# One norm recorded ahead of attention, the last pairs' products in another order, and new planned costs for narrow matmuls, merges and norm sums

## The chip, the cores and the metric

The kernel runs on one core of a Trainium2 chip. The metric is the device time of one execution, in microseconds. The engines named here are TensorE (PE in the profile, its weight loads PEld), VectorE (DVE), ScalarE (ACT), GpSimd (POOL) and SyncE (SP), which issues the DMAs.

## The reference

A network of two layers on 1024 tokens with 1024 features, all in f32. Layer 0 mixes by attention over a sliding window of 128 tokens with a sink per head (16 query heads and 4 key heads of 64), layer 1 by an HGRN2 recurrence in chunks of 64 tokens (8 heads of 128). Each layer ends with an MLP of 4096 hidden features with a squared ReLU, and each part starts with an RMS norm.

```python
def rmsnorm(x, gain):
    xf = x.astype(jnp.float32)
    y = xf * lax.rsqrt(jnp.mean(jnp.square(xf), axis=-1, keepdims=True) + NORM_EPS)
    return (y * gain.astype(jnp.float32)).astype(x.dtype)

def sqrelu_mlp(h, w_up, w_down):
    return jnp.square(jax.nn.relu(h @ w_up)) @ w_down

    scores = jnp.where(mask[None, :, None, None], scores, NEG_INF)
    m = jnp.maximum(jnp.max(scores, axis=-1, keepdims=True), sink)
    e = jnp.exp(scores - m)
    probs = e / (jnp.sum(e, axis=-1, keepdims=True) + jnp.exp(sink - m))
    ...
        scores = jnp.einsum('bhtd,bhtsd,bhsd->bhts', qc, decay, kc)
        o_intra = jnp.einsum('bhts,bhse->bhte', scores, vc)
        new_state = jnp.exp(b_last)[..., None] * state + jnp.einsum(
            'bhsd,bhse->bhde', kc * jnp.exp(b_last[:, :, None, :] - b), vc)
        return new_state, o_inter + o_intra
    ...
    for layer in range(DEPTH):
        j = layer // N_MIXERS
        h = rmsnorm(x, mix_norm[layer])
        if layer % N_MIXERS == 0:
            y = sliding_window_attention(h, positions, attn_w_qkv[j], attn_b_qkv[j],
                                         attn_sinks[j], attn_w_o[j])
        else:
            y = hgrn2_recurrence(h, lbs[layer], hgrn_w_in[j], hgrn_g_norm[j], hgrn_w_o[j])
        x = x + y.astype(x.dtype)
        h = rmsnorm(x, mlp_norm[layer])
        x = x + sqrelu_mlp(h, mlp_w_up[layer], mlp_w_down[layer]).astype(x.dtype)
    return rmsnorm(x, final_norm)
```

## The kernel before, in words

**Work.** The tokens are held as two halves of 512, the features as 8 tiles of 128. A matmul of f32 data is three passes (`mm3`): each operand is split into a high part and a rest (tiles `wh` and `wl` of a weight, pairs of `a` of an activation), and high x high, high x rest and rest x high are summed in one PSUM bank. A split is a cast (on ScalarE or VectorE) and a subtraction (VectorE). PSUM has eight banks in two pools of four, `p` and `q`. Raw weights arrive in tiles `wr`, their sums stand in `m`, activations in `a` and `t`, small columns in `sm`.

**Order.** Every operation is first recorded in `Schedule` by `add` and only then issued. `due` (line 187) walks backward from the end and gives each operation a rank by its due time; `order` (line 205) then runs a list schedule: each engine, when free by the planned clock, takes the ready operation of the lowest rank. The planned clock is made of the cost that each operation is recorded with (`mm`, line 426, plans n * rate / 2.4 + 3 ns), a table of latencies between engines, and 120 ns where TensorE changes from whole matmuls to column matmuls. `lead` lets what is recorded under it rank earlier by 120 ns for each unit; `LEAD` is 100, so 12 us. A buffer of a pool is given to the next tile in recorded order when it is free by the plan. What results is one program per engine, which that engine works through in order. All operations are issued by one helper, so every line of the profile is L372, and tiles tell them apart.

**The MLP.** `pair` (line 643) takes two of the 16 steps of the upper product at a time, by seven products instead of eight (the rows and columns are combined first, in the way of Strassen). Each `product` is 12 matmuls of 128x512 for the half pair's tile. Products 1, 6, 7 and 4 add up in the bank main, 5 and 3 in the bank side (both of pool `q`), 2 alone in own (pool `p`). Between 1, 6, 7 and 4 the bank main is read (`read`, a copy into a `t` tile): u1, u2, u3; p5 is read from side. The hidden tiles that result are stored in DRAM. `down` (line 731) then loads them again (`t<-d`), splits them and multiplies them by the lower weights, three matmuls to a bank, eight banks in turn. Its first matmuls are free to go ahead of the last pair's last product.

**Attention.** `attention` (line 1059) scales and splits the first half, records its keys, values and queries (`qkv`), then the second half's scaling, and then `attend(0)` interleaved with `qkv(1)`. `scaled` returns the split tiles and a function that, when called, records the norm: eight squares (ScalarE), their sum (VectorE), and `token_rstd` (line 492): matmuls of the sum by a column of 1/1024, one for each block of 128 tokens (128x1 in the trace), the root on ScalarE, and some small VectorE operations. `qkv(1)` calls it at its first step.

**HGRN.** `recurrence` (line 1245) works on pairs of tokens' blocks inside a chunk, by levels: `products` (line 1269) issues narrow matmuls (32 or 64 columns wide) on halves of the array's columns, and `merge` (line 1278) puts their result into the scores by a predicated copy on VectorE.

Of the kernel before, what the change touches and what calls it, by code (L numbers as in the profile page):

```python
# [18 lines left out]
P = 128  # L19
# [6 lines left out]
MT = FF // P  # L26
# [9 lines left out]
BPH = NBLK // NH  # L36
# [6 lines left out]
CH = 64  # L43
# [93 lines left out]
LEAD = 100  # L137
# [181 lines left out]
class Net:  # L319
# [172 lines left out]
    def token_rstd(self, acc, inner=1.0, outer=1.0, n=TH, tag="q"):  # L492

        ps = self.psum(tag)
        nb = n // P
        for j in range(nb):
            self.mm(ps[:, j : j + 1], acc[:, j * P : j * P + P], self.mean, True, True, 64, 4)
        v, y, z = (self.t(F32, (P, BPH), "sm")[:, :nb] for _ in range(3))
        self.ts("DVE", v, ps[:, :nb], inner, EPS, ALU.mult, ALU.add, 4)
        self.act(y, v, AF.Sqrt, 4)  # L500
        self.op("DVE", self.nc.vector.reciprocal, [y], [y], 100, y, y)
        self.tt("DVE", z, y, y, ALU.mult, 4)
        self.tt("DVE", z, z, v, ALU.mult, 4)
        self.ts("DVE", z, z, -0.5 * outer, 1.5 * outer, ALU.mult, ALU.add, 4)
        self.tt("DVE", y, y, z, ALU.mult, 4)
        return y
# [136 lines left out]
    def pair(self, m, x):  # L643

        w = self.strassen_weights(*(self.io["up"][self.layer, i] for i in (m, m + MT // 2)))

        def read(ps):
            z = self.t()
            self.take(z, ps)
            return z  # L650

        main, side, own = self.psum("q"), self.psum("q"), self.psum()
        self.product(main, w[1], x[1], True)
        u1 = read(main)
        self.product(own, w[2], x[2], True)
        self.product(side, w[5], x[5], True)
        p5 = read(side)
        self.product(main, w[6], x[6], False)
        u2 = read(main)
        self.product(side, w[3], x[3], False)  # L660
        self.product(main, w[7], x[7], False)
        u3 = read(main)
        self.product(main, w[4], x[4], False)
        def kept(name, z):
            self.hid[name, m] = self.keep(z)

        self.add_bank(u1, own)
        h00 = self.square_relu(u1)
        kept(1, h00)
        self.add_bank(u2, side)  # L670
        h01, t5, t6, t4 = self.square_relu(u2), *(self.t() for _ in range(3))
        self.tt("any", t5, h01, h00, ALU.subtract)
        kept(5, t5)
        self.tt("any", p5, p5, u3, ALU.add)
        h11 = self.square_relu(p5)
        kept(3, h11)
        self.tt("any", t6, h11, t5, ALU.subtract)
        kept(6, t6)
        self.tt("any", h01, h11, h01, ALU.subtract)
        kept(7, h01)  # L680
        h10 = self.square_relu(main, True)
        kept(2, h10)
        self.tt("any", t4, h10, t6, ALU.subtract)
        kept(4, t4)
# [374 lines left out]
    def attention(self, layer):  # L1059
        self.v, self.dv, self.ks, self.kl = [], [], [None] * 3, [None] * 3  # L1060
        self.q = [[None] * 2 for _ in range(NBLK)]
        out = [{}, {}]
        self.load_x([0])
        h = [self.scaled(layer, 0)]
        self.attention_constants()
        run(self.qkv(0, *h[0]))
        self.load_x([1])
        h.append(self.scaled(layer, 1))
        interleave(self.attend(0, out[0]), self.qkv(1, *h[1]), 16, 24)
        interleave(self.attend(1, out[1]), self.o_proj(0, out[0]), 24, 8)  # L1070
        self.mlp_first(layer)
        run(self.o_proj(1, out[1]))
# [172 lines left out]
    def recurrence(self, e, ready, totals, out):  # L1245

        gates = ready.pop(e)
        NC = NH * BPH
        chunk = lambda z, j: z[:, j * CH : j * CH + CH]
# [4 lines left out]
        def parts(z, lg):  # L1254
            return z.rearrange("p (n a h) -> p n a h", a=2, h=1 << lg)

        def moved(lg):
            return [(k, [parts(chunk(q, j), lg)[:, :, 1] for j in range(2 * BPH)]) for q, f, k, g in gates]
# [10 lines left out]
        def products(part, operands, late, width=CH // 2):  # L1269
            part = part.rearrange("p (c t) -> p c t", c=NC)  # L1270
            for hf, (k, qs) in enumerate(operands):
                for c in range(BPH):
                    for b in range(2):
                        rows = slice(b * CH, b * CH + CH)
                        j = 2 * c + b
                        self.mm(part[rows, hf * BPH + c], chunk(k, j), qs[j], True, True, width, 2.06, "columns", late)

        def merge(part, lg):
            H = 1 << lg
            n = CH // (2 * H)  # L1280
            mask = parts(self.level_mask[lg], lg)[:, :, 1].unsqueeze(1).to_broadcast([P, NC, n, H])
            target = scores.rearrange("p c (n a h) -> p c n a h", a=2, h=H)[:, :, :, 1]
            part = part.rearrange("p (c n h) -> p c n h", c=NC, n=n)
            self.op("DVE", self.nc.vector.copy_predicated, [target], [mask, part], 70 + NC * CH // 2 * 1.04, target, mask, part)

        def views(operands):
            return [z for k, qs in operands for z in (k, *qs)]
# [8 lines left out]
        gates = decayed  # L1296
        late = views(plain) + views(moved(0))
        products(whole, plain, late, CH)
        products(half, moved(0), late)
        mask = self.diag.unsqueeze(1).to_broadcast([P, NC, CH])  # L1300
        self.tt("DVE", scores, whole.rearrange("p (c t) -> p c t", c=NC), mask, ALU.mult)
        merge(half, 0)
        yield
        for lg in range(1, LEVELS, 2):
# [5 lines left out]
            if lg < LEVELS - 1:  # L1310
                second = moved(lg + 1)
                late = views(first) + views(second)
                products(low, first, late)
                products(high, second, late)
                merge(low, lg)
                merge(high, lg + 1)
            else:
                late = views(first) + [z for q, f, k, g in gates for z in (q, k)]
                products(low, first, late)
                cross = self.psum("q")[:CH].rearrange("p (c t) -> p c t", c=NC)  # L1320
                for hf, (q, f, k, g) in enumerate(gates):
                    for c in range(BPH):
                        self.mm(cross[:, hf * BPH + c], chunk(k, 2 * c), chunk(q, 2 * c + 1), True, True, CH, 3.9, "columns", late)
                merge(low, lg)
                weights = []
                for hf in range(NH):
                    s, c = self.t(F32, (P, BPH, 2, CH)), slice(hf * BPH, hf * BPH + BPH)
                    self.memset(s[CH:, :, 0].only(0), 0.0, "Pool")
                    self.copy(s[:CH, :, 0].only(1), scores[:CH, c], 4 * CH)
                    self.copy(s[CH:, :, 1].only(2), scores[CH:, c], 4 * CH)  # L1330
                    self.copy(s[:CH, :, 1].only(3), cross[:, c], 4 * CH)
                    weights.append(s)
                at, tot = self.double(CH, gates, tot, tots, at)
# [149 lines left out]
def run(pieces):  # L1483
    for _ in pieces:
        pass


def interleave(main, other, n_main, n_other):
    done = 0
    for k, _ in enumerate(main):  # L1490
        while done * n_main < (k + 1) * n_other and next(other, run) is not run:
            done += 1
    run(other)
# [81 lines left out]
```

## Time and profile before

| | us |
|---|---|
| runs: 2004.93, 2006.69, 2010.59; median | 2006.69 |
| the profiled execution | 2007.87 |
| its span | 2005.5 |
| around the span | 2.37 |
| TensorE busy | 1979.5 |
| VectorE busy | 1699.2 |
| ScalarE busy | 1013.7 |
| mean granted clock of TensorE | 0.998 |

A row of the timeline gives start, length, engine, line, operation, the tile written, the tiles read, their shape, how many in a row, and in brackets the engine's idle time just ahead and who released it. Numbers behind tiles are left out there. A matmul's length in the trace is longer than the step from one to the next, since they overlap.

### The profile page before, as it was taken

The numbers are of one execution on the slowest core, as the hardware profiler recorded it, in microseconds if no ns is written. First come the engines' busy times: TensorE is split into PE (matmuls) and PEld (weight loads), VectorE is DVE, ScalarE is ACT, GpSimd is POOL, SyncE is SP. The second block draws the span as 40 slices with busy tenths as digits, with TensorE's granted clock in tenths as the row PEclk, the third lists the DMA queues.
The fourth block names the chain that finished last, engine by engine and source line by source line (L and its number), as shares of the span: only waits on it lengthen the run. The fifth ranks groups of instructions, "written<-read, shape, count | busy, mean of one in ns | idle before, by whom it ended". The sixth has DMA issues, their size and how long they took to land.

```text
span 2005.5 us, 32701 instructions
## 1 busy us (share of the span) xinstructions
PE 1979.5 (99%) x11404; PEld 1718.5 (86%) x11404; DVE 1699.2 (85%) x3360; ACT 1013.7 (51%) x2045; POOL 62.7 (3%) x124
## 2 busy tenths in 40 slices
PE   9999999999999999999999999999999999999998
PEld 8877788888888888888888888888888888888887
DVE  8999899777778878799898999989977777887787
ACT  6567796554454323255345555554654445323352
POOL 4030100000000000000000000000000000000001
PEclk9999999999999999999999999999999999999999
DMA  6212463544468967745422212667444446886752
GB/s 216 90 53 59 127 222 120 184 167 160 146 204 292 314 217 264 235 163 176 146 63 78 78 59 90 207 208 244 142 167 160 146 162 237 286 301 215 236 179 85
DMA packets 196677, 345.88 MB, mean 172 GB/s; under 512 B 21536, under 2 KB 31776, under 8 KB 196512
## 3 DMA queue, kind: packets, MB, share of 16 engines
q1 hardware_dynamic: 195936, 343.28, 52.0%
q8 instruction: 89, 1.46, 0.3%
q14 instruction: 76, 0.62, 0.1%
q10 hardware_dynamic: 576, 0.52, 0.1%
HBM read 250.39 MB, written 93.32 MB: 171 GB/s over the span
## 4 chain that ended last, share of the span: by engine, by line
PE 85%; DVE 7%; DMA 3%; issue 2%; ACT 2%; POOL 0%; SPq 0%; POOLq 0%; DVEq 0%; ACTq 0%
PE q L372 51%; PE p L372 34%; DVE t L372 3%; DVE a L372 2%; DVE wl L372 1%; ACT t L372 1%; ACT a L372 1%; DMA wr<-in_down 1%; DVE m L372 0%; DMA a<-in_x 0%; ACT wh L372 0%; ACT m L372 0%; DMA t<-d 0%; DMA wr<-in_wqkv 0%; DMA wr<-in_wv 0%
## 5 line engine op out<-in xcount | busy, mean ns | idle before, releaser
L372 PE MATMUL q<-a,wh 128*128 128x512 f32 x2560 | 761.8, 379 | 3.5 <-ACT t L372 3.5
L372 PE MATMUL p<-a,wh 128*128 128x512 f32 x2112 | 644.6, 383 | 0.1
L372 PEld LDWEIGHTS q<-a,wh 128*128 128x128 f32 x2560 | 482.3, 189 | 74.1 <-ACT t L372 5.0
L372 PE MATMUL q<-a,wl 128*128 128x512 f32 x1280 | 484.9, 379 | 0.0
L372 PEld LDWEIGHTS p<-a,wh 128*128 128x128 f32 x2112 | 394.2, 189 | 54.6 <-issue 1.2
L372 PE MATMUL p<-a,wl 128*128 128x512 f32 x1056 | 401.6, 381 | 0.0
L372 ACT CAST a<-t 128x512 fp32r<-128x512 f32 x283 | 172.0, 619 | 286.0 <-PE q L372 142.8
L372 PEld LDWEIGHTS q<-a,wl 128*128 128x128 f32 x1280 | 241.9, 189 | 34.3
L372 ACT ACTIVATE t<-t 128x512 f32<-128x512 f32 x272 | 171.1, 631 | 189.8 <-DVE t L372 182.2
L372 DVE TENSOR_TENSOR wl<-wr,wh 128x512 fp32r<-128x512 f32 x352 | 240.6, 686 | 11.7 <-ACT wh L372 3.9
L372 DVE TENSOR_TENSOR t<-t,t 128x512 f32<-128x512 f32 (+3 forms) x364 | 224.9, 638 | 26.8 <-ACT t L372 23.1
L372 PEld LDWEIGHTS p<-a,wl 128*128 128x128 f32 x1056 | 199.7, 189 | 26.8 <-issue 0.4
L372 DVE TENSOR_TENSOR a<-t,a 128x512 fp32r<-128x512 f32 (+1 forms) x326 | 217.2, 685 | 6.4 <-ACT a L372 6.0
L372 DVE TENSOR_TENSOR wl<-m,wh 128x512 fp32r<-128x512 f32 x248 | 170.5, 689 | 16.7 <-ACT wh L372 10.1
L372 ACT COPY t<-q 128x512 f32<-128x512 f32 (+2 forms) x214 | 119.4, 560 | 112.6 <-PE q L372 111.5
L372 ACT CAST wh<-wr 128x512 fp32r<-128x512 f32 x173 | 106.5, 618 | 100.2 <-PE p L372 45.7
L372 DVE TENSOR_TENSOR m<-wr,wr 128x512 f32<-128x512 f32 x160 | 110.0, 689 | 39.7 <-DMA wr<-in_down 24.0
L372 DVE CAST wh<-wr 128x512 fp32r<-128x512 f32 x179 | 76.5, 427 | 78.9 <-PE q L372 47.2
L372 ACT CAST wh<-m 128x512 fp32r<-128x512 f32 x154 | 94.8, 618 | 57.2 <-PE q L372 35.1
L372 PE MATMUL p<-wh,a 128*128 128x512 f32 x352 | 110.9, 385 | 0.0
L372 PEld LDWEIGHTS q<-t,t 128*64 128x64 f32 (+1 forms) x2160 | 95.2, 144 | 14.0 <-issue 5.3
L372 PE MATMUL q<-t,t 128*64 128x32 f32 (+2 forms) x2160 | 104.1, 229 | 1.8 <-DVE t L372 1.3
(130 smaller groups left out, 2056.8 us busy)
## 6 DMA issues: line engine op xcount, KB each, us to landing
d<-t SPq DMA_DIRECT2D x276, 256.0 KB, 2.8
t<-d SPq DMA_DIRECT2D x264, 256.0 KB, 4.5
wr<-in_down SPq DMA_DIRECT2D x256, 256.0 KB, 3.9
wr<-in_up SPq DMA_DIRECT2D x128, 256.0 KB, 2.9
a<-d SPq DMA_DIRECT2D x60, 256.0 KB, 5.1
wr<-in_wqkv SPq DMA_DIRECT2D x48, 256.0 KB, 3.0
d<-a SPq DMA_DIRECT2D x48, 256.0 KB, 3.5
wr<-in_win SPq DMA_DIRECT2D x48, 256.0 KB, 2.9
```

What stands on the lines that cost most here:

```text
L372: fn(*[place(a) for a in args], **{k: place(v) for k, v in kw.items()})
```

## The change

Five edits, none of which adds or takes away an operation of the network:

1. `token_rstd` plans its matmuls at rate 9 instead of 4 (243 instead of 110 ns each).
2. In the last pair of a layer (m == 15) the products are issued as 1, 5, 6, 2, 7, 3, 4; all other pairs keep 1, 2, 5, 6, 3, 7, 4. The reads of main and side follow the same products as before.
3. The second half's norm is recorded ahead of `attend(0)`, under a lead of 200, so it ranks 24 us earlier than without; `qkv(1)` is handed the finished column.
4. `products` plans narrow matmuls at rate 3.6 where they are 32 wide (51 instead of 31 ns) and 2.4 where 64 wide (67 instead of 58).
5. `merge` plans 300 ns more for the first two levels (636 instead of 336).

```diff
@@ -494,7 +494,7 @@
         ps = self.psum(tag)
         nb = n // P
         for j in range(nb):
-            self.mm(ps[:, j : j + 1], acc[:, j * P : j * P + P], self.mean, True, True, 64, 4)
+            self.mm(ps[:, j : j + 1], acc[:, j * P : j * P + P], self.mean, True, True, 64, 9)
         v, y, z = (self.t(F32, (P, BPH), "sm")[:, :nb] for _ in range(3))
         self.ts("DVE", v, ps[:, :nb], inner, EPS, ALU.mult, ALU.add, 4)
         self.act(y, v, AF.Sqrt, 4)
@@ -650,17 +650,14 @@
             return z
 
         main, side, own = self.psum("q"), self.psum("q"), self.psum()
-        self.product(main, w[1], x[1], True)
-        u1 = read(main)
-        self.product(own, w[2], x[2], True)
-        self.product(side, w[5], x[5], True)
-        p5 = read(side)
-        self.product(main, w[6], x[6], False)
-        u2 = read(main)
-        self.product(side, w[3], x[3], False)
-        self.product(main, w[7], x[7], False)
-        u3 = read(main)
-        self.product(main, w[4], x[4], False)
+        got = {}
+        for name in (1, 5, 6, 2, 7, 3, 4) if m == MT // 2 - 1 else (1, 2, 5, 6, 3, 7, 4):
+            ps = main if name in (1, 6, 7, 4) else own if name == 2 else side
+            self.product(ps, w[name], x[name], name in (1, 2, 5))
+            if name in (1, 5, 6, 7):
+                got[name] = read(ps)
+        u1, p5, u2, u3 = (got[name] for name in (1, 5, 6, 7))
+
         def kept(name, z):
             self.hid[name, m] = self.keep(z)
 
@@ -1066,6 +1063,10 @@
         run(self.qkv(0, *h[0]))
         self.load_x([1])
         h.append(self.scaled(layer, 1))
+        self.s.lead = 2 * LEAD
+        r = h[1][1]()
+        self.s.lead = 0
+        h[1] = h[1][0], lambda: r
         interleave(self.attend(0, out[0]), self.qkv(1, *h[1]), 16, 24)
         interleave(self.attend(1, out[1]), self.o_proj(0, out[0]), 24, 8)
         self.mlp_first(layer)
@@ -1273,7 +1274,7 @@
                     for b in range(2):
                         rows = slice(b * CH, b * CH + CH)
                         j = 2 * c + b
-                        self.mm(part[rows, hf * BPH + c], chunk(k, j), qs[j], True, True, width, 2.06, "columns", late)
+                        self.mm(part[rows, hf * BPH + c], chunk(k, j), qs[j], True, True, width, 3.6 if width < CH else 2.4, "columns", late)
 
         def merge(part, lg):
             H = 1 << lg
@@ -1281,7 +1282,7 @@
             mask = parts(self.level_mask[lg], lg)[:, :, 1].unsqueeze(1).to_broadcast([P, NC, n, H])
             target = scores.rearrange("p c (n a h) -> p c n a h", a=2, h=H)[:, :, :, 1]
             part = part.rearrange("p (c n h) -> p c n h", c=NC, n=n)
-            self.op("DVE", self.nc.vector.copy_predicated, [target], [mask, part], 70 + NC * CH // 2 * 1.04, target, mask, part)
+            self.op("DVE", self.nc.vector.copy_predicated, [target], [mask, part], 70 + NC * CH // 2 * 1.04 + 300 * (lg < 2), target, mask, part)
 
         def views(operands):
             return [z for k, qs in operands for z in (k, *qs)]
```

The planned costs and the record order set each engine's program. Four places of it follow; tiles carry their record number, which differs between the two programs.

**The last pair of layer 0, on TensorE.** Here main is q_6780, and the weight tiles name the product: wh_6845 is product 7, wh_6876 product 4, wh_6822 product 3. The banks q_7003 and q_7013 are the first of `down`. Before, from product 7's last matmuls on:

```order
L372 MATMUL q_6780<-a_4114,wh_6845 128x512
L372 MATMUL q_6780<-a_4214,wh_6845 128x512
L372 MATMUL q_6780<-a_4114,wl_6861 128x512
L372 MATMUL q_7003<-a_6827,wh_6909 128x512
L372 MATMUL q_7003<-a_6841,wh_6909 128x512
L372 MATMUL q_7003<-a_6827,wl_6919 128x512
L372 MATMUL q_7013<-a_6827,wh_6909 128x512
L372 MATMUL q_7013<-a_6841,wh_6909 128x512
L372 MATMUL q_7013<-a_6827,wl_6919 128x512
L372 MATMUL q_6780<-a_4120,wh_6876 128x512
L372 MATMUL q_6780<-a_4219,wh_6876 128x512
```

and after, the end of product 7 with the start of product 3 (whose side bank is q_6839), then its end:

```order
L372 MATMUL q_6780<-a_4106,wh_6845 128x512
L372 MATMUL q_6780<-a_4199,wh_6845 128x512
L372 MATMUL q_6780<-a_4106,wl_6861 128x512
L372 MATMUL q_6839<-a_3893,wh_6822 128x512
L372 MATMUL q_6839<-a_4145,wh_6822 128x512
L372 MATMUL q_6839<-a_3893,wl_6834 128x512
```

```order
L372 MATMUL q_6839<-a_4089,wh_6822 128x512
L372 MATMUL q_6839<-a_4166,wh_6822 128x512
L372 MATMUL q_6839<-a_4089,wl_6834 128x512
L372 MATMUL q_6780<-a_4029,wh_6876 128x512
L372 MATMUL q_6780<-a_4208,wh_6876 128x512
L372 MATMUL q_6780<-a_4029,wl_6892 128x512
```

Product 3's twelve matmuls now stand between products 7 and 4, and the six of `down` come behind product 4.

**The same place on ScalarE.** The copies out of q_6780 are the reads u2 and u3; a<-t casts are splits for `down`, ACTIVATE t<-t a ReLU and its square. Before:

```order
L372 COPY t_6940<-q_6780 128x512
L372 CAST a_6952<-t_6921 128x512
L372 CAST a_6962<-t_6929 128x512
L372 CAST wh_6974<-wr_6749 128x512
L372 ACTIVATE t_6989<-t_6940 128x512
L372 ACTIVATE t_6989<-t_6989 128x512
L372 CAST wh_7001<-m_6802 128x512
L372 COPY t_7009<-q_6780 128x512
```

and after:

```order
L372 COPY t_6910<-q_6780 128x512
L372 CAST a_6947<-t_6919 128x512
L372 ACTIVATE t_6956<-t_6852 128x512
L372 ACTIVATE t_6956<-t_6956 128x512
L372 CAST wh_6969<-wr_6749 128x512
L372 COPY t_6978<-q_6780 128x512
```

Between the reads of u2 and u3 two casts less stand in ScalarE's program; one split, the ReLU with its square and one weight cast are left.

**The end of the first half's keys, on VectorE and TensorE.** The fourth block's keys are rotated into t_502 (before) and t_508 (after); q_173 is the bank whose last read is SCALAR_TENSOR_TENSOR a<-q_173. VectorE before:

```order
L372 SCALAR_TENSOR_TENSOR a_574<-q_167,sm_339,a_302 128x256
L372 TENSOR_TENSOR t_73<-q_549,a_106 64x128
L372 TENSOR_TENSOR a_586<-a_574,a_536 128x256
L372 TENSOR_TENSOR t_88<-q_549,a_109 64x128
L372 SCALAR_TENSOR_TENSOR a_574<-q_173,sm_339,a_302 128x256
L372 TENSOR_TENSOR t_93<-q_549,a_114 64x128
```

and after:

```order
L372 SCALAR_TENSOR_TENSOR a_576<-q_167,sm_333,a_288 128x256
L372 SCALAR_TENSOR_TENSOR a_576<-q_173,sm_333,a_288 128x256
L372 TENSOR_TENSOR t_73<-q_550,a_106 64x128
L372 TENSOR_TENSOR a_595<-a_576,a_539 128x256
L372 TENSOR_TENSOR t_88<-q_550,a_109 64x128
L372 TENSOR_TENSOR a_595<-a_576 128x256
```

The read of q_173 now follows that of q_167 directly. TensorE before (q_607 takes the transposes of t_502):

```order
L372 MATMUL p_519<-wl_407,a_155 128x512
L372 MATMUL q_590<-c_79,t_494 128x128 x2
L372 MATMUL p_519<-wh_395,a_171 128x512
L372 MATMUL p_485<-wh_410,a_191 128x512
L372 MATMUL p_485<-wl_425,a_191 128x512
L372 MATMUL p_485<-wh_410,a_230 128x512
L372 MATMUL q_607<-c_79,t_502 128x128 x2
```

and after (q_597 takes those of t_508):

```order
L372 MATMUL p_525<-wh_393,a_155 128x512
L372 MATMUL q_587<-c_79,t_497 128x128 x2
L372 MATMUL p_525<-wl_408,a_155 128x512
L372 MATMUL q_597<-c_79,t_508 128x128 x2
L372 MATMUL p_525<-wh_393,a_171 128x512
L372 MATMUL p_494<-wh_434,a_191 128x512
```

The transposes stand three matmuls earlier.

**The second half's norm, on TensorE and ScalarE.** The 128x1 matmuls write the four means. TensorE before, in the midst of the scores:

```order
L372 MATMUL q_1116<-a_106,a_1029 128x256
L372 MATMUL q_1116<-a_106,a_1077 128x256
L372 MATMUL q_1116<-t_73,a_1029 128x256
L372 MATMUL q_1116<-t_73,a_1077 128x256
L372 MATMUL q_1122<-c_71,t_847 128x1 x4
L372 MATMUL p_1034<-wh_950,a_673 128x512
L372 MATMUL p_1043<-wh_950,a_515 128x512
```

and after, at the end of the first half's projections (q_798 is the last of their banks):

```order
L372 MATMUL q_790<-wl_900,a_285 128x512
L372 MATMUL q_790<-wh_885,a_352 128x512
L372 MATMUL q_798<-wh_885,a_285 128x512
L372 MATMUL q_987<-c_71,t_847 128x1 x4
L372 MATMUL q_798<-wl_900,a_285 128x512
L372 MATMUL q_798<-wh_885,a_352 128x512
L372 MATMUL q_1000<-c_79,a_764 128x128
```

ScalarE before (sm_1143 is the root, m_372 the first scores under the exponential):

```order
L372 COPY m_372<-q_1106 128x2x128
L372 COPY m_372<-q_1116 128x2x128
L372 ACT_TABLE_LOAD
L372 ACTIVATE sm_1143<-sm_1137 128x4
L372 COPY m_375<-q_1132 128x2x128
L372 COPY m_375<-q_1135 128x2x128
L372 CAST wh_1157<-wr_960 128x512
L372 ACT_TABLE_LOAD
L372 ACTIVATE m_372,sm_1164<-m_372,sm_1150 128x129 x4
```

and after (sm_1019 is the root):

```order
L372 ACTIVATE t_916<-a_559 128x512
L372 CAST wh_1006<-wr_910 128x512
L372 ACT_TABLE_LOAD
L372 ACTIVATE sm_1019<-sm_1002 128x4
L372 ACTIVATE a_1022<-q_1000 64x512
L372 ACTIVATE a_1031<-q_1012 64x512
L372 ACTIVATE a_1040<-q_1026 64x512
```

The first of the two table loads and the root now stand ahead of the copies of the transposed queries (a<-q), where they stood between the copies of the first scores.

## The prediction, made before the changed kernel ran

> **What bounds the kernel.** I began with the page: busy shares, then the chain that ended last.
>
> ```profile
> PE 1979.5 (99%) x11404; PEld 1718.5 (86%) x11404; DVE 1699.2 (85%) x3360; ACT 1013.7 (51%) x2045; POOL 62.7 (3%) x124
> PE 85%; DVE 7%; DMA 3%; issue 2%; ACT 2%; POOL 0%; SPq 0%; POOLq 0%; DVEq 0%; ACTq 0%
> ```
>
> TensorE is busy for 1979.5 of the span's 2005.5 us, so it idles for 26.0 us. The change issues the same matmuls, so it can win only idle time or lose some more. The view of waits, for PE, says who is waited for (total us, times, longest):
>
> ```profile
> PE q L372 <- DVE t L372: 6.6, 7, 1.9
> PE q L372 <- DVE a L372: 4.3, 9, 1.1
> PE q L372 <- ACT t L372: 3.7, 3, 2.3
> PE q L372 <- DVE m L372: 1.9, 3, 1.3
> PE q L372 <- ACT m L372: 0.7, 1, 0.7
> ```
>
> Those are 17.2 us. The busy time by stage (stretch, its length, PE busy with its records, then the other engines, clock, DMA share) places them:
>
> ```profile
> 0.00:40.00 40.00, 37.23 (x172) 31.46 (x173) 33.92 (x114) 27.44 (x55) 13.19 (x37) 1.00 0.75 251
> 40.00:130.00 90.00, 86.29 (x466) 71.84 (x465) 82.19 (x208) 47.30 (x136) 28.09 (x43) 1.00 0.27 80
> 590.00:615.00 25.00, 23.74 (x110) 20.36 (x109) 22.67 (x40) 16.97 (x30) 0.00 (x0) 1.00 0.93 307
> 615.00:850.00 235.00, 235.00 (x1090) 205.80 (x1089) 191.50 (x334) 75.39 (x127) 0.00 (x0) 1.00 0.79 262
> 1000.00:1340.00 340.00, 337.41 (x3351) 295.69 (x3350) 307.64 (x726) 185.72 (x369) 8.04 (x18) 1.00 0.32 103
> 1690.00:1710.00 20.00, 17.75 (x82) 14.96 (x81) 17.12 (x30) 9.81 (x17) 0.00 (x0) 1.00 0.87 309
> 1960.00:2005.50 45.50, 36.41 (x279) 34.84 (x277) 33.11 (x83) 12.28 (x28) 5.35 (x6) 0.90 0.26 93
> ```
>
> The first 130 us lose 2.77 + 3.71 us, the two seams from the last pair to the down products 1.26 and 2.25, the recurrence 2.59, the end 9.09 (there the order stays). A pure stage gives the price of one matmul: 235.00 us / 1090 = 0.216 us, so a product of 12 takes 2.59 us. The granted clock is 1.00 in all stages but the last.
>
> **Part 1: the last pairs.** Product 4 adds to the bank main, so it waits until ScalarE has read what product 7 left there. ScalarE, then TensorE, at the seam of layer 0 (start, length, operation, how many together, in brackets the idle time ahead and who ended it):
>
> ```profile
> 601.62 1.28 ACT L372 CAST a<-t 128x512 fp32r<-128x512 f32 x2 [1.64 <-DMA t<-d]
> 602.80 0.62 ACT L372 CAST wh<-wr 128x512 fp32r<-128x512 f32 x1
> 604.76 1.29 ACT L372 ACTIVATE t<-t 128x512 f32<-128x512 f32 x2 [1.34 <-DVE t L372]
> 605.96 0.60 ACT L372 CAST wh<-m 128x512 fp32r<-128x512 f32 x1
> 606.47 0.58 ACT L372 COPY t<-q 128x512 f32<-128x512 f32 x1
> 605.45 0.38 PE L372 MATMUL q<-a,wl 128*128 128x512 f32 x1
> 607.09 0.70 PE L372 MATMUL q<-a,wh 128*128 128x512 f32 x2 [1.26 <-ACT t L372]
> ```
>
> and at that of layer 1:
>
> ```profile
> 1691.73 1.29 ACT L372 CAST a<-t 128x512 fp32r<-128x512 f32 x2 [2.65 <-DMA t<-d]
> 1696.56 0.58 ACT L372 COPY t<-q 128x512 f32<-128x512 f32 x1
> 1694.56 0.38 PE L372 MATMUL q<-a,wl 128*128 128x512 f32 x1
> 1697.19 0.70 PE L372 MATMUL q<-a,wh 128*128 128x512 f32 x2 [2.25 <-ACT t L372]
> ```
>
> The COPY is the read; PE follows 0.04 us after it ends (606.47 + 0.58 = 607.05). Before, six matmuls of the down products (6 x 0.216 = 1.30 us) stood between product 7 and product 4. The last of them began at 605.45 and 1694.56, so product 4 could have begun at 605.67 and 1694.78; it lost 1.42 and 2.41 us, 3.83 together.
>
> After, product 3 stands between them and the six down matmuls behind product 4. Product 4's slot is then 1.30 us earlier: 607.09 - 1.42 - 1.30 = 604.37, and 1693.48. The read would be covered by 2.59 us, were it not for ScalarE's own queue: ahead of it still stand one split (it waits for the transfer t<-d), a ReLU with its square, and one weight cast. With the transfer as it is: 601.62 + 0.65 + 1.2 + 0.55 + 0.58 = 604.6, so product 4 loses 0.27 instead of 1.42: **1.15 us** won. In layer 1: 1691.73 + 0.68 + 1.2 + 0.55 + 0.58 = 1694.75, a loss of 1.29 instead of 2.41: **1.12 us**. Sum **2.3**. Bounds: 3.83 if the transfers land early enough, 0 if the reads end where they do now. What is late next is the transfer: SyncE's queue holds this load at the same place as before, and only the loads after it go ahead of a store. The down matmuls behind product 4 have their operands, since they ran ahead of it until now.
>
> **Part 2: the first keys.** TensorE and VectorE at the end of the first keys:
>
> ```profile
> 37.07 0.41 PE L372 MATMUL q<-c,t 128*128 128x128 f32 x2 [1.13 <-DVE a L372]
> 33.95 0.48 DVE L372 SCALAR_TENSOR_TENSOR a<-q,sm,a 128x256 f32<-128x256 f32 x1
> 35.50 0.28 DVE L372 TENSOR_TENSOR t<-q,a 64x128 fp32r<-64x128 f32 x1 [1.07 <-ACT a L372]
> 36.44 0.48 DVE L372 SCALAR_TENSOR_TENSOR a<-q,sm,a 128x256 f32<-128x256 f32 x1
> ```
>
> The transposes at 37.07 need the bank that the operation at 36.44 frees, and this stands behind one that waits 1.07 us for ScalarE. In the new order it goes directly behind that of 33.95, so it ends at 33.95 + 2 x 0.45 = 34.85. The transposes move three matmuls (0.65 us) ahead to a slot near 35.1 and find the bank free. Of the 1.13 us I take **0.9**, since VectorE, 82.19 of the next 90 us busy, may claim some of it back. Bounds: 1.13, and -0.65 if the earlier slot is too early.
>
> **Part 3: the norm ahead.** ScalarE around the second half's norm, and TensorE:
>
> ```profile
> 66.99 0.63 ACT L372 ACTIVATE t<-a 128x512 f32<-128x512 f32 x1 [0.57 <-DVE t L372]
> 73.13 0.62 ACT L372 CAST wh<-wr 128x512 fp32r<-128x512 f32 x1 [5.51 <-PE q L372]
> 84.79 1.28 ACT L372 ACT_TABLE_LOAD   x1
> 86.49 0.20 ACT L372 ACTIVATE sm<-sm 128x4 f32<-128x4 f32 x1 [0.41 <-DVE sm L372]
> 87.82 1.28 ACT L372 ACT_TABLE_LOAD   x1
> 89.11 0.40 ACT L372 ACTIVATE m<-m,sm 128x129 f32<-128x129 f32 x1
> 84.20 0.95 PE L372 MATMUL q<-c,t 128*128 128x1 f32 x8
> 91.85 0.63 PE L372 MATMUL q<-c,m 128*128 128x128 f32 x4 [0.73 <-ACT m L372]
> ```
>
> The square sums end near 68 us, yet their matmuls stood at 84.20. They now stand two matmuls ahead of the end of the projection, near 72.5, with some 4 us of slack; the first table load and the root fall into ScalarE's idle 5.51 us. That takes 1.28 + 0.41 + 0.20 = 1.9 us from ScalarE ahead of the exponentials at 89.11; the second load stays. The step issues no DMA; the eight squares and their additions were done early before, too, so the matmuls, the root and six small VectorE operations are all that moves. The wait of 0.73 us at 91.85 goes, if VectorE brings the scores sooner. I take **0.5**; bounds 0.73 and, if the early matmuls find the sums late, -0.65 (three matmuls' time).
>
> The Trainium skill, "ScalarE: Activation LUTs", section "What ACT_TABLE_LOAD costs", gives a switch 1283 ns and 1380 ns of drain. The rows agree with the load, but show no drain: the load of 87.82 ends at 89.10 and the exponential begins at 89.11. By the page's sum two switches would take 5.3 us; by the rows 2.6.
>
> **Part 4: the planned rates.** The three planned costs (norm sums 4 to 9, narrow matmuls, merges +300 ns) remove and add nothing on the chip. Their effect is a reordering of single groups. The places where norm sums (128x1) wait or barely don't:
>
> ```profile
> 317.94 1.05 PE L372 MATMUL q<-c,t 128*128 128x1 f32 x8 [0.96 <-DVE t L372]
> 316.00 2.49 DVE L372 TENSOR_TENSOR t<-t,t 128x512 f32<-128x512 f32 x4
> 909.33 1.02 PE L372 MATMUL p<-c,t 128*128 128x1 f32 x8
> ```
>
> At 317.94 the sums now stand three matmuls (0.65 us) earlier, at 909.33 four (0.86 us), at about 1062 three (0.65 us); VectorE's last addition is one or two operations earlier too (0.62 us each, 2.49 / 4). I put all of it at a loss of **0.3**, near zero as the two shifts nearly cancel; bounds: the sum of the three, 2.2 us lost, and 0.96 won. In the recurrence the narrow matmuls keep their groups; its whole idle time is 2.59 us. I take 0, bounds 2.6 won (all idle gone) and 2.6 lost (as much again).
>
> **Sum**: 2.3 + 0.9 + 0.5 - 0.3 = 3.4 us. The profiled execution took 2007.87 us (its span of 2005.5 and 2.37 around it), so 2004.5; the median of the runs shown, 2006.69, lies 1.18 below it, so the forecast is **2003.3 us**.
>
> **Rivals.**
> (A) The reads stay as late, since ScalarE's queue waits for t<-d (1.64 and 2.65 us there now) and the transfers land later in the new order. Part 1 is then 0: 2005.6. For it: DMA shares of 0.93 and 0.87. Against: the transfers' order is nearly the same.
> (B) VectorE swallows parts 2 and 3 (82.19 of 90 us busy): only 2.3 - 0.3 remain, 2004.7.
> (C) All waits touched go: 3.83 + 1.13 + 0.73 + 0.96 + 2.59 = 9.2: 1997.5. Against: ScalarE's queue in part 1.
> (D) Slower: TensorE takes its queue in order, so a norm sum's matmuls set before their sum is there hold all behind them. Price: 2.2 us for the three places and 2.6 in the recurrence, 4.8 against the 3.7 won: 1.1 slower, 2007.8. It decides from the point where the sums come more than 3.7 us late in all; with (A) as well, 2010.1. For it: 317.94 waits already.
> (E) The order changes and the time doesn't, because TensorE is 99% busy and what one place wins the next wait takes: 2006.7.
> (F) Each table switch holds ScalarE for 1.38 us beyond its load. One lies in the idle 5.51 us, the other delays the exponentials: 1.4 us lost, 2004.7. The gap of 0.01 us behind the load speaks against it. It is the drain of the Trainium skill's page "ScalarE: Activation LUTs", section "What ACT_TABLE_LOAD costs".
>
> **Chances**: forecast 0.42, A 0.12, B 0.14, C 0.12, D 0.12, E 0.06, F 0.02. A measurement of this kernel tells about 0.3% (6 us) from no change. Faster by more needs under 2000.7: C, and the forecast's own tail, 0.05 if part 1 and the recurrence both come out at their upper bounds: 0.17. Slower by more needs over 2012.7: half of D, had it also a loss in the seams: 0.06. Same 0.77. The range reaches from (C)'s upper half, 1998.5, to (D) with (A) less a little, 2009.5.
>
> **What would show it.** Right: PE's wait for "ACT t" falls from 3.7 us to about 1.5; the wait at 37.07 is gone; no PE wait for "ACT m" near 92; a table load near 70. Wrong: new waits for DVE ahead of a 128x1 matmul (D), or the read of main still ending 2.6 us after product 7 has been followed by product 3 (A). A time under 2000.7 would mean that the recurrence gained, which I put at nothing.

## The result, and the profile after

| | before | changed |
|---|---|---|
| median, us (4 runs each) | 2008.64 | 2019.91 |
| the profiled execution, us | 2007.87 | 2021.16 |
| its span, us | 2005.5 | 2019.2 |

The ratio is 1.0055, 95% interval 1.0043 to 1.0068: some 11 us slower, where 3.4 us faster was forecast, and outside the range given.

The page of the changed kernel, busy shares and the chain that ended last:

```profile
PE 1985.1 (98%) x11404; PEld 1721.7 (85%) x11404; DVE 1702.6 (84%) x3367; ACT 1008.5 (50%) x2038; POOL 59.1 (3%) x124
PE 70%; DVE 15%; DMA 6%; issue 4%; ACT 3%; SPq 0%; POOL 0%; DVEq 0%; POOLq 0%; ACTq 0%
```

The matmuls are as many as before. TensorE's idle time rose from 26.0 to 34.1 us (2019.2 - 1985.1), and its busy time by 5.6 us, though it does the same. VectorE's share of the chain doubled. The waits of TensorE (total, times, longest):

```profile
PE q L372 <- DVE t L372: 9.2, 13, 1.9
PE q L372 <- DVE a L372: 5.0, 8, 2.0
PE q L372 <- DVE m L372: 3.7, 4, 1.4
PE q L372 <- DVE sm L372: 3.6, 3, 1.6
PE q L372 <- ACT t L372: 1.8, 3, 0.9
```

"ACT t" fell from 3.7 to 1.8 us, near the 1.5 forecast, but by luck: product 4, for which that was forecast, waits in neither layer, and the rest stands at other places, 0.94 of it at 406.91 and 0.76 at 612.42, where nothing waited before. The waits for VectorE rose. The busy time by stage (the same columns as before):

```profile
0.00:40.00 40.00, 36.37 (x171) 30.74 (x172) 33.24 (x111) 27.17 (x54) 11.55 (x36) 1.00 0.75 251
40.00:130.00 90.00, 85.43 (x460) 71.21 (x459) 82.72 (x209) 47.06 (x135) 27.47 (x44) 1.00 0.27 80
590.00:615.00 25.00, 24.24 (x113) 20.93 (x112) 22.16 (x39) 16.94 (x31) 0.00 (x0) 1.00 0.90 302
1000.00:1340.00 340.00, 332.11 (x3304) 290.41 (x3303) 303.94 (x718) 178.88 (x356) 7.75 (x18) 0.99 0.31 99
1690.00:1710.00 20.00, 20.00 (x94) 17.23 (x93) 17.64 (x31) 12.45 (x23) 0.00 (x0) 1.00 0.88 293
```

The recurrence lost most: 7.89 us idle where it had 2.59, 47 records fewer in the same stretch, and a mean clock of 0.99. The seams gained, the first 130 us lost 0.86 + 0.86. A look into the recurrence, first TensorE around its longest stall, then VectorE, then TensorE's stretches by time:

```profile
1281.33 1.27 PE L372 MATMUL q<-t,t 128*64 128x32 f32 x36
1283.95 0.82 PE L372 MATMUL q<-t,t 128*64 128x32 f32 x18 [1.35 <-DVE m L372]
1284.70 1.22 PE L372 MATMUL p<-a,wh 128*128 128x512 f32 x2
1281.85 0.73 DVE L372 COPY_PREDICATED t<-c,q 128x256 f32<-128x256 int32 x1
1283.17 0.73 DVE L372 COPY_PREDICATED t<-c,q 128x256 f32<-128x256 int32 x1
1283.68 0.22 DVE L372 TENSOR_TENSOR m<-m 128x8 f32<-128x8 f32 x1
```

```profile
1280.00:1284.00 4.00, 2.65 (x54) 2.13 (x52) 3.90 (x13) 1.98 (x5) 0.56 (x2) 1.00 0.91 319
1284.00:1288.00 4.00, 4.00 (x26) 3.31 (x27) 3.62 (x13) 1.75 (x4) 0.00 (x0) 0.57 0.89 286
```

A row of narrow matmuls stops in its midst and goes on at 1283.95, 0.05 us after the predicated copy (a `merge`) of 1283.17 has ended (1283.90). The view puts the wait down to "DVE m", the operation that ended at the same time; the merge is the one that reads this PSUM bank. Over the next 4 us, 1284 to 1288, the mean clock is 0.57. Nine such stops stand in the changed kernel; each ends 0.05 to 0.06 us after a merge. The kernel before has two, more than half of its 2.59 us of idle time in the recurrence:

```profile
1065.79 0.42 PE L372 MATMUL q<-t,t 128*64 128x32 f32 x6 [0.82 <-DVE t L372]
1282.33 0.54 PE L372 MATMUL q<-t,t 128*64 128x32 f32 x12 [0.53 <-DVE t L372]
```

From the first narrow matmul to the last, the recurrence takes 312.85 us in the changed kernel (1018.76 to 1331.61) and 305.51 before (1015.80 to 1321.31): 7.3 us more.

The program tells why. `recurrence` lets a bank hold two halves, low and high. `products` fills low, then high; `merge(low)` may follow as soon as low is done, by the planner's books, because low and high are booked apart. But the bank is one tile where the waits are set: if the merge of low is issued before the last matmuls of high, those wait for its end. The high half of one group on TensorE, with its waits (DVE is VectorE, the number its semaphore's), before:

```
L372 MATMUL q_14466<-t_14325,t_14318 64x32 [waits DVE_49]
L372 MATMUL q_14466<-t_14325,t_14318 64x32 x7
L372 MATMUL q_14466<-t_14336,t_14310 64x32 [waits DVE_49]
L372 MATMUL q_14466<-t_14336,t_14310 64x32 x7
```

and after:

```
L372 MATMUL q_14468<-t_14323,t_14310 64x32 [waits DVE_49]
L372 MATMUL q_14468<-t_14323,t_14310 64x32 x6
L372 MATMUL q_14468<-t_14323,t_14310 64x32 [waits DVE_49]
L372 MATMUL q_14468<-t_14334,t_14318 64x32 x8
```

Before, the second wait stands where a new operand begins. After, it stands one matmul ahead of that, and is a wait for the merge. Such a group is called broken below: a merge of its bank is issued before its last matmul. That can be counted in the program before it runs.

### The profile page after: what moved, and what is told of

It is laid out like the page before. It is cut to its first block, busy times and chain, and to the rows that moved or that the text cites. A ratio compares the mean times of both kernels' runs of the same rounds, so it can differ in the third digit from the quotient of the medians.

```text
span 2019.2 us, 32703 instructions
## 1 busy us (share of the span) xinstructions
PE 1985.1 (98%) x11404; PEld 1721.7 (85%) x11404; DVE 1702.6 (84%) x3367; ACT 1008.5 (50%) x2038; POOL 59.1 (3%) x124
## 4 chain that ended last, share of the span: by engine, by line
PE 70%; DVE 15%; DMA 6%; issue 4%; ACT 3%; SPq 0%; POOL 0%; DVEq 0%; POOLq 0%; ACTq 0%
PE q L372 45%; PE p L372 25%; DVE t L372 7%; DVE a L372 4%; DMA wr<-in_down 3%; DVE wl L372 2%; ACT t L372 2%; DMA t<-d 2%; DVE m L372 1%; ACT a L372 1%; DMA wr<-in_up 1%; ACT wh L372 1%; DMA t<-v 0%; DMA wr<-in_wv 0%; DVE wh L372 0%
```

## The experiments

Theory 1: the planned rates put merges inside groups of the same bank, and each broken group costs TensorE the merge. Theory 2: the norms (edits 1 and 3) cost it, as rival D had it. "Over" below is against the kernel before; all kernels of a batch ran on one chip. Edit 5 alone was not run.

| kernel | broken groups | ratio to before | 95% interval |
|---|---|---|---|
| before | 2 | 1 | |
| the change | 9 | 1.0055 | 1.0043 to 1.0068 |
| edit 4 alone | 16 | 1.0126 | 1.0097 to 1.0155 |
| change without edit 4 | 3 | 1.0017 | 1.0006 to 1.0028 |
| change with link | 0 | 0.9999 | 0.9986 to 1.0013 |
| edits 2 and 3 | 2 | 0.9984 | 0.9974 to 0.9995 |
| edit 2 alone | 2 | 0.9988 | 0.9979 to 0.9998 |
| link, without edit 1 | 0 | 0.9980 | 0.9970 to 0.9989 |
| edits 2, 3 and link | 0 | 0.9981 | 0.9971 to 0.9990 |
| change, two banks | 0 | 1.0008 | 0.9999 to 1.0018 |
| edit 1 alone | 4 | 1.0030 | 1.0018 to 1.0042 |
| edit 3 alone | 2 | 0.9996 | 0.9985 to 1.0007 |
| edit 4, two banks | 0 | 1.0000 | 0.9991 to 1.0010 |

**Edit 4 alone**

```diff
-  self.mm(part[rows, hf * BPH + c], chunk(k, j), qs[j], True, True, width, 2.06, "columns", late)
+  self.mm(part[rows, hf * BPH + c], chunk(k, j), qs[j], True, True, width, 3.6 if width < CH else 2.4, "columns", late)
```

> The kernel before with edit 4 alone (planned rates of the narrow matmuls). In its program 16 groups of narrow matmuls have a merge recorded inside them that reads the other half of their bank (2 in the kernel before, 9 in the changed one). Theory 1 (what stands behind such a merge in the bank waits for its end, some 0.8 us each): 14 more such groups, 9 to 13 us slower than before, with 16 stalls inside narrow groups that end 0.05 us after a merge. Theory 2 (norm sums set too early, or the norm moved ahead, make the loss): within 2 us of before.

Slower by 1.26%, some 25 us, twice what was expected. TensorE's longest group of waits in the recurrence (1000 to 1345 us), then the recurrence by busy time:

```profile
PE q L372 <- DVE t L372: 15.0, 16, 1.7
1000.00:1345.00 345.00, 328.60 (x3234) 285.08 (x3233) 299.76 (x695) 174.13 (x343) 7.83 (x18) 0.98 0.29 93
```

Sixteen waits for sixteen broken groups. Counted from one matmul's start to the next, the stops add 17.7 us here, 7.6 in the changed kernel and 1.7 before: about 0.85 to 1.1 us each. The expectation took 0.8 us for a stop, where these come to 1.1 each, and it lacked the clock: behind four of the stops 24 large matmuls step by 0.427 instead of 0.216 us, 5.1 us more. 16.0 (17.7 - 1.7) and 5.1 are most of the loss.

**The change without edit 4** (the line above taken back)

> The changed kernel without edit 4: 3 such groups instead of 9. Theory 1: 5 to 8 us faster than the changed kernel (6 x 0.8, and the slow clock after the longest stall), so 3 to 6 us slower than before. Theory 2: as slow as the changed kernel, 11 us over before.

1.0017: 3.4 us over before, 7.6 under the changed kernel (1.0055 - 1.0017). Theory 1 holds here, too. What is left over before isn't the three broken groups alone (2.4 us by the same count, against 1.7 in the kernel before). The mean clock is 0.50 in two stretches, 84.18 to 87.59 and 1026.26 to 1029.67, where the kernel before has 1.00. The second stands behind one of the three stops (0.82 us, to 1025.61), the first behind a wait of 2.00 us for VectorE in the attention.

**The change with a link in the planner**

```diff
-        def merge(part, lg):
+        def merge(part, lg, rest=()):
...
-            self.op("DVE", self.nc.vector.copy_predicated, [target], [mask, part], 70 + NC * CH // 2 * 1.04 + 300 * (lg < 2), target, mask, part)
+            self.op("DVE", self.nc.vector.copy_predicated, [target], [mask, part, *rest], 70 + NC * CH // 2 * 1.04 + 300 * (lg < 2), target, mask, part)
...
-                merge(low, lg)
+                merge(low, lg, [high])
```

> The changed kernel, with one input added to the planner's record of merge(low): the bank's other half. The planned costs stay; only the plan knows that this merge and the other half's matmuls exclude each other. No group is broken. Theory 1: the stalls inside narrow groups are gone (9 before), 7 to 10 us faster than the changed kernel, 1 to 4 us slower than before or level with it. Theory 2: as slow as the changed kernel.

0.9999: the stops are gone, and so is the whole loss, 11 us. From the first narrow matmul to the last it is now 304.21 us (1016.61 to 1320.82), 8.6 less than in the changed kernel; the rest of the 11 lies outside, where the link moves the plan as well, and was not located. The waits in the recurrence, and its idle time, 3.08 us:

```profile
PE q L372 <- DVE sm L372: 1.6, 1, 1.6
1000.00:1345.00 345.00, 341.92 (x3371) 298.92 (x3370) 312.95 (x738) 186.78 (x370) 7.75 (x18) 1.00 0.33 105
```

No wait for "DVE t" stands in the view. The costs planned for narrow matmuls and merges stayed in; the harm is not in them, but in what the planner doesn't know. The run with the link and without edit 1, below, which keeps both costs and is 0.9980, bears this out.

**Edits 2 and 3 alone, then edit 2 alone** (the diffs of `attention` and `pair` above)

> The kernel before with edits 2 and 3 alone (last pairs' order, norm ahead); the broken groups stay at 2. By parts 1 to 3 of the prediction: 2 to 4 us faster than before. If the loss came from the norm ahead (theory 2): slower than before by 3 us or more.

> The kernel before with edit 2 alone (the last pairs' order). Part 1 of the prediction: 2.3 us faster, 3.8 at most, 0 if ScalarE's reads end as late as now. If the run with edits 2 and 3 had its gain from the norm ahead instead: level with before here.

0.9984 and 0.9988, that is 3.2 and 2.4 us faster. The pairs' new order does what part 1 said. Edit 2 alone, the waits for ScalarE's reads, then the first matmuls of product 4 of layer 0, of the fourth bank of its `down`, and of product 4 of layer 1:

```profile
PE q L372 <- ACT t L372: 0.9, 3, 0.4
603.60 0.59 PE L372 MATMUL q<-a,wh 128*128 128x512 f32 x2
608.70 0.70 PE L372 MATMUL q<-a,wh 128*128 128x512 f32 x2 [0.41 <-ACT t L372]
1691.79 0.70 PE L372 MATMUL q<-a,wh 128*128 128x512 f32 x2 [0.35 <-ACT t L372]
```

Product 4 doesn't wait in layer 0 and waits 0.35 us in layer 1. The 0.41 us are new: `down` now follows product 4 directly, and its fourth bank, of the pool of main and side, waits for the last read of main.

**The link without edit 1** (norm sums planned at rate 4, the rest of the change and the link as above)

> The changed kernel with the link (as in the run with the link), without edit 1: norm sums planned at rate 4 again. If edit 1 is what keeps the run with the link level with before (its norm sums set at other places near 80 and at 1345 us): 2 to 3 us faster than that run, 2003.5 to 2005. If the planned cost of merges or narrow matmuls does that: no faster than it.

0.9980 against 0.9999 with edit 1: about 3.8 us, a little more than expected, though the two intervals just touch, so this size is rough; that edit 1 costs time is shown by the run of it alone, below. Two places show it. With edit 1 (the changed kernel), ScalarE and TensorE at the norm ahead, and TensorE at the last norm of the recurrence:

```profile
72.71 0.97 PE L372 MATMUL q<-c,t 128*128 128x1 f32 x8
74.94 1.28 ACT L372 ACT_TABLE_LOAD   x1
76.46 3.89 ACT L372 ACTIVATE a<-q 64x512 fp32r<-64x512 f32 x7
84.24 0.46 PE L372 MATMUL q<-a,a 128*128 128x256 f32 x2 [2.01 <-DVE a L372]
1347.35 1.13 PE L372 MATMUL q<-c,sm 128*128 128x128 f32 x8 [1.58 <-DVE sm L372]
```

and without it, with the link:

```profile
65.08 1.28 ACT L372 ACT_TABLE_LOAD   x1
73.86 0.59 ACT L372 ACTIVATE a<-q 64x512 fp32r<-64x512 f32 x1
82.55 0.46 PE L372 MATMUL q<-a,a 128*128 128x256 f32 x2 [0.68 <-DVE a L372]
1331.00 1.13 PE L372 MATMUL q<-c,sm 128*128 128x128 f32 x8
```

At rate 9 the plan sets the table load behind a weight cast, so it runs at 74.94 and pushes the copies of the transposed queries from 73.86 to 76.46. The first scores then wait 2.01 instead of 0.68 us; with the link and edit 1 they wait 2.01 us, too, and a stretch of halved clock follows. At 1347.35 the spread of the root's column waits 1.58 us, without edit 1 not at all. A third place, 0.94 us at 406.91 in the upper products of layer 0, came with edit 1 too; why was not tried.

**Edits 2 and 3 with the link**

> The kernel before with edits 2 and 3 and the link in the planner: no broken groups, old planned costs. Theory 1: 1.7 us faster than the run with edits 2 and 3 (its two broken groups gone), 3 to 4 us faster than before, the fastest of all. Rival: the plan's other moves swallow that, level with the run of edits 2 and 3.

0.9981, 3.8 us faster, as expected; with the one above the fastest. Against edits 2 and 3 alone (0.9984, another batch) the link's 1.7 us can't be told apart, as the intervals overlap.

**The halves in a bank each**

```diff
-            bank = self.psum("q")
-            low, high = bank[:, : NC * CH // 2].only(0), bank[:, NC * CH // 2 :].only(1)
+            low, high = (self.psum("q")[:, : NC * CH // 2] for _ in range(2))
```

The first run is the changed kernel with this edit, the second the kernel before with edit 4 and this edit.

> The changed kernel with the two halves of narrow matmuls in a bank each, instead of two halves of one bank. Nine merges still stand in the program inside the other half's group. Theory 1, that what waits is a write to the bank that the merge reads: no stalls inside narrow groups, 6 to 10 us faster than the changed kernel, unless the fourth bank of pool q is missed elsewhere. Rival, that TensorE waits for any merge set there: the nine stalls stay.

> The kernel before with edit 4 alone, but the two halves of narrow matmuls in a bank each. 16 merges stand inside the other half's group, as in the run with edit 4 alone, which was 26 us slower than before. Theory 1 (the shared bank is what waits): no stalls inside groups, no slow clock behind them, within 4 us of before. Rival (the planned rate harms by the places it gives): 10 us slower or more.

1.0008 and 1.0000, where the same costs with a shared bank gave 1.0055 and 1.0126, and no row of narrow matmuls stops. The recurrence of the first, then of the second:

```profile
1000.00:1345.00 345.00, 341.05 (x3368) 298.60 (x3367) 311.71 (x739) 184.75 (x368) 7.75 (x18) 1.00 0.32 103
1000.00:1345.00 345.00, 341.06 (x3367) 297.97 (x3366) 313.26 (x732) 186.95 (x371) 7.75 (x18) 1.00 0.33 105
```

3.95 us are idle instead of 7.89 (345 - 337.11 over the same 345 us in the changed kernel), and 3.94 instead of 16.40. But the expectations were wrong in one point: the plan moved with the banks, so the merges don't stand where they stood. By the traces a merge of low begins before the last matmul of high 6 times in the first run and 4 times in the second, not 9 and 16 times. Those 6 and 4 are the test. Here is the same merge in the changed kernel, and then with two banks, each with its matmuls:

```profile
1024.40 1.36 PE L372 MATMUL q<-t,t 128*64 128x32 f32 x40
1026.60 0.89 PE L372 MATMUL q<-t,t 128*64 128x32 f32 x24 [0.83 <-DVE t L372]
1025.81 0.73 DVE L372 COPY_PREDICATED t<-c,q 128x256 f32<-128x256 int32 x1
```

```profile
1023.36 2.06 PE L372 MATMUL q<-t,t 128*64 128x32 f32 x64
1024.66 0.73 DVE L372 COPY_PREDICATED t<-c,q 128x256 f32<-128x256 int32 x1
```

With two banks the row of narrow matmuls runs on through the merge. So it is the tile that the merge and the matmuls share that makes TensorE wait. That the places themselves do no harm is shown for those 6 and 4 merges alone, and the two ratios mix both: no shared bank, and fewer merges inside a group. Whether the chip could do without the wait in a shared bank the runs don't show.

**Edit 1 alone, edit 3 alone**

> The kernel before with edit 1 alone (norm sums planned at rate 9). Four broken groups instead of 2 (2 x 0.8 us), and the last norm of the recurrence stands as in the changed kernel, where TensorE waited 1.58 us for its root's column: 2.5 to 4 us slower than before. If edit 1 hurts only together with the norm ahead: within 1.5 us of before.

> The kernel before with edit 3 alone (the norm ahead, old planned rates). Part 3 of the prediction: 0.5 us faster (from 0.7 faster to 0.65 slower). The table load stands far ahead of the copies of the queries here. If the norm ahead is harmful by itself: 2 us slower or more.

Edit 1 alone: 1.0030, 6 us over, more than expected. Its two further broken groups cost 1.7 us by the count above; four waits of it are these:

```profile
93.93 0.63 PE L372 MATMUL q<-c,m 128*128 128x128 f32 x4 [1.45 <-DVE m L372]
101.15 0.63 PE L372 MATMUL q<-c,m 128*128 128x128 f32 x4 [0.81 <-DVE m L372]
408.29 0.70 PE L372 MATMUL q<-a,wh 128*128 128x512 f32 x2 [0.88 <-ACT t L372]
1344.00 1.13 PE L372 MATMUL q<-c,sm 128*128 128x128 f32 x8 [1.58 <-DVE sm L372]
```

The first is 0.7 us more than the wait for the exponentials had before; the other three are new. Other waits rose and fell by less than 1.3 us each, so the loss is spread over the plan and has no single place. Edit 3 alone: 0.9996, within its interval no change, so half a microsecond can neither be shown nor refuted; its table load runs at 65.55, far ahead of the copies.

## Why the prediction was wrong, point by point

- **Part 4, the planned rates, failed, and with it the forecast.** Of the recurrence it said: "In the recurrence the narrow matmuls keep their groups; its whole idle time is 2.59 us. I take 0, bounds 2.6 won (all idle gone) and 2.6 lost (as much again)." The groups do keep their places on TensorE. What moved is the merge, on VectorE, past matmuls of its own bank on TensorE, and the prediction looked at each engine's order by itself. With narrow matmuls planned at 51 instead of 31 ns, the group of high lasts longer in the plan, so more merges of low come due within it; that is argued from the planner, and the counts agree (16 groups with edit 4 alone, 9 with all five edits, where merges are planned 300 ns longer, too). Seven more broken groups cost 5.9 us (7.6 - 1.7), the slow clock behind one of them 1.7 (4.00 us at 0.57); together 7.6, about the 7.3 us by which the stretch of narrow matmuls grew, which is gone with the link. Twice the idle time of before was no bound, for nothing in it counts how many groups could break. Two of the waits that made up the 2.59 us were already of this kind (0.82 at 1065.79, 0.53 at 1282.33), and the prediction didn't ask what they were.
- **The same part's term for the norm sums was far too small.** It put them at a loss of 0.3, from three places. At the first, the wait fell (0.96 before, 0.57 at 318.23), at the second there is none, and near the third, "about 1062", the trace before has no 128x1 matmul. The loss came elsewhere: edit 1 costs some 3.8 us with the link and 6 alone. With the 7.6 us above, 3.5 here, and the 1.4 that parts 2 and 3 didn't win, 12.5 of the 14.4 us between forecast and result are named; the rest stays open.
- **Part 1, the last pairs, was right in its mechanism and its sum**: 2.3 us forecast, 2.4 measured alone (0.4 to 4.2 by the interval). That the sum fits so well is partly luck, as the shares are not those forecast. Of product 4's waits 0 and 0.35 us remain, where 0.27 and 1.29 were forecast, and the wait of 0.41 us at the fourth bank of `down` was not forecast at all; so layer 0 won 0.85 and layer 1 1.90. In the changed kernel the split that waits for the transfer still stands ahead of the read, as forecast. ScalarE there, layer 1, where product 4 begins right behind the read, at 1708.13, with no wait in the view:

```profile
1705.28 0.62 ACT L372 CAST a<-t 128x512 fp32r<-128x512 f32 x1 [4.25 <-DMA t<-d]
1707.50 0.58 ACT L372 COPY t<-q 128x512 f32<-128x512 f32 x1
```

- **Part 2, the first keys, brought nothing of its 0.9 us.** The wait at 37.07 is gone, as forecast, but one of nearly its length stands at the transposes before it:

```profile
33.87 0.41 PE L372 MATMUL q<-c,t 128*128 128x128 f32 x2 [1.05 <-DVE a L372]
```

- **Part 3, the norm ahead, was wrong in one step**: "the first table load and the root fall into ScalarE's idle 5.51 us". The order quoted in the section on the change has a weight cast ahead of the load, and the idle stretch of the profile ended with a weight cast that waited for TensorE: the load could not run before it. In the change it ran at 74.94, behind that stretch, and cost more than it brought. The wait of 0.73 us at 91.85 that was to go stood as one of 0.66 at 92.83, now for VectorE. With the old rate the load stands ahead of the cast, and the step does no harm, and no gain that can be measured.
- **Rival D** had the right sign and the wrong mechanism. The norm sums' own matmuls did not wait more; what waited were the copies and the spread behind them.
- **The chance of 0.06 for slower by over 0.3%** came from D alone. That planned costs nearer to the traced ones could make a worse plan was not among the rivals.

## What to carry to other kernels

Compare orders across engines, not each by itself: for every buffer that two engines share, count whose operation on it is issued inside the other's run. The count (2, 9, 16, 3, 0, 4) gave the number of stops in the recurrence exactly. It didn't give their price: with 16 the loss was twice what was expected, for the stops were longer and the clock fell behind four of them. A list schedule that books parts of a buffer apart must do so only where the waits are set apart as well; where they aren't, better costs can make the plan worse, and the mending is a dependency, not a cost.

## What the runs showed of the hardware that was not expected

A stop of TensorE of 0.8 to 2 us is sometimes followed by about 3.4 us in which its granted clock is halved, and large matmuls step by 0.427 instead of 0.216 us. It happened behind one of nine stops in the changed kernel (0.57 over 1284 to 1288), four of sixteen with edit 4 alone, one of three without edit 4, and twice in the attention (without edit 4 at 84.18, with the link at 83.71), where the work isn't narrow matmuls. One of those four, behind the 3.4 us ahead of it (the last column but two is the clock):

```profile
1110.12:1113.54 3.42, 1.78 (x55) 1.63 (x51) 3.42 (x11) 0.60 (x2) 0.56 (x2) 1.00 0.27 71
1113.54:1116.95 3.41, 3.41 (x8) 2.67 (x9) 3.01 (x9) 1.14 (x2) 0.00 (x0) 0.50 0.30 88
```

No length of a stop decides it: one of 0.82 us (to 1025.61, without edit 4) brought it, while stops of 1.40 and 1.39 us (to 1067.09 and 1250.42, edit 4 alone) and a wait of 2.01 us (to 84.24, the changed kernel) went without. The four halved stretches with edit 4 alone begin at 1113.54, 1157.91, 1205.70 and 1297.86 and last 3.41 us each; their distances are 13, 14 and 27 times that length, as if they stood on a fixed grid. So it seems to count, too, where on that grid a stop falls, and how much TensorE does in the rest of that stretch; this was not tried.

The Trainium skill, "TensorE: Matmul & The Clock Gate", section "Part 1: The HAM clock gate", describes a gate that drops to half speed after an idle window of about 3.4 us, and a window that runs free. The halved step, the 3.4 us and the grid agree with it. A wholly idle window was not needed here, as TensorE was busy for 1.78 of the 3.42 us ahead of the halved stretch above. What the gate counts as activity the runs don't show.
